# Hybrid decoder block in fp32: the beginning and the end of the FFN's down product in another order, with other raw buffers

## The chip, the cores and the metric

The kernel runs on one core of a Trainium2 chip. The metric is the device time of one execution in microseconds (us). The engines are named as the profile names them: PE (TensorE, matmuls), PEld (its weight loads, which overlap the matmuls), DVE (VectorE), ACT (ScalarE), POOL (GpSimd, here nearly only an issuer of DMAs) and SP (SyncE, which issues DMAs only). [...]

## What is computed

A decoder block for one sequence of 512 tokens with 2048 channels: RMSNorm with a shift and scale from a conditioning vector, two token mixers in parallel (a gMLP gate and a sparse attention), a gated sum, and then a dense SwiGLU FFN. Only the FFN matters here (5632 hidden channels):

```python
h = rms_norm(x1, g_pre_ffn) * (1 + scale) + shift
hid = silu(h @ w_ffn_gate) * (h @ w_ffn_up)          # (512, 5632)
ffn = hid @ w_ffn_down                               # (512, 2048)
out = x1 + gate * rms_norm(ffn, g_post_ffn)
```

## The kernel before

**Arithmetic.** [...] Each operand is divided into a high part `h` (a CAST on ACT) and a low part `l` (a subtraction on DVE), and a product is three matmuls: low by high, high by high, high by low. `split` does that, and the trace shows it as `wh<-...` on ACT (L95) and `wl<-...` on DVE (L79). Both products of the FFN use one level of Strassen's scheme, so that seven quarter products take the place of eight; the sums of quarters that it needs are made on DVE ("fix") and on a few tensors that go through DRAM.

**Steps.** The work of the FFN is a list, `plan`, of `Step`s. A step has a source (`src`, one or two DMA loads of up to 512 KB into a raw buffer, issued on SP), perhaps a `fix` (additions on DVE in the raw buffer), the division into `wh` and `wl`, and the matmuls (`mm`). Hooks place work between steps: `pre` and `post` before and after a step, `late` one step later. `run` walks through the list. Before it emits the matmuls of step i it emits loads and divisions of the steps up to i + `ahead`, and the loads of the steps up to i + `far`; the fix of a step comes two steps before its division. Each engine executes its instructions in the order in which `run` emits them, so `ahead` says what stands in front of what on DVE and ACT:

```python
            for j in range(i, i + st.ahead + 1):
                if st.far:
                    for q in range(i, j + 3):
                        load(q)
                    prefix(j + 2)
                load(j)
                divide(j)
```

**Buffers.** `fetch` gives each step a raw buffer: `wraw`, `xraw` or `draw`, three of each, in a cycle. `divide` does the same for `wh` and `wl`. The `draw` buffers lie in the pool of the down product, which takes the space of operands of the Strassen units before it.

**The FFN's stages.** Unit 0 is computed by `fill`, units 1 to 10 by `strassen(u)`: each makes 512 hidden channels, in four tiles `hn` (tiles 0 and 1, then 2 and 3). Sums of a unit's hidden channels are needed by the down product. `hid_out` transposes the `hn` tiles on PE into a PSUM bank, and `hid_sums` copies from there on ACT (L1523, L1524) and makes four sums on DVE; `sa` and `sb` go to DRAM. For the units 0 to 9 that is done inside the next unit; for the last it is done inside the first steps of the down product, by `mm2` of p = 0 and by the hook `hid_last`.

`down(v)` runs for v = 0 and 1, each a half of the output columns. Its first part has 22 groups p of three steps: `srca` (the hidden sums `sa`), `src1` with `mm1` (weights; fix of two additions with the rows of the third step; result bank A, and B) and `src2` with `mm2` (banks D and C). A group is 24 matmuls of 128 x 512. At the start the order on PE is `mm1` of p = 0 into bank A (6 matmuls), `mm2` of p = 0 into D (6), the 16 transposes of the last unit's `hn` into B and C, `mm1` of p = 1 (6), `mm2` of p = 1 (6), and then the 24 products into B and C of both groups that had been left out. The fix also stores one sum to DRAM (`t2`, by POOL). The second part has 11 groups m of five steps (two loads of `sb`, `mm3` into A, `mm4` into D, `mm5` into C). With the last of them each bank is complete; `late_a`, `late_d` and `post_c` square it on ACT, scale it by `frow` on DVE (`frow` is the FFN's gate row, broadcast to all partitions), and, for v = 1, `d_end` finishes a token tile: the reciprocal root, four multiply-adds of 128 x 512 (`fo<-fo,rd,x`, L86) and the stores of the output. In the last tile the order is A, D, C.

The names of tiles in the trace: `st` is a PSUM bank, `sa_d`, `sb_d`, `t_d`, `t2` are tensors in DRAM, `in_w_dn_dram` the down weights, `in_w_gu_dram` those of gate and up, `gg_d` the gate row.

## Time and profile before

| | before |
|---|---|
| median of three runs | 2617.68 us (2616.56 to 2618.94) |
| profiled execution, own time | 2617.31 us |
| profiled execution, span | 2615.5 us |
| mean granted TensorE clock | 0.992 |
| PE busy | 2546.6 us (97%), 11493 matmuls |
| DVE, ACT busy | 1951.4 us (75%), 1142.7 us (44%) |

The profiled execution's own time is 1.81 us more than its span, which is what lies around the first and last instruction. Starts in the rows below are us from the span's start; the down product begins at about 2158.5 us and ends at 2599.3 us on PE, and the first Strassen unit after `fill` begins at about 1373 us.

### The profile page before, as it was taken

What the parts mean: (1) busy time and instruction counts of PE and PEld (TensorE: products, weight loads), DVE (VectorE), ACT (ScalarE), POOL (GpSimd) and SP (SyncE); (2) the same over time, 40 slices, a digit from 0 to 9 for tenths busy, and PEclk for the clock granted to TensorE, in tenths of its full rate; (3) what the DMA queues carried; (4) which work ended last, traced back from release to release, by engine and by line L of the source; (5) the groups of instructions that cost most, each with busy time, mean ns of one, the idle gap of its engine ahead of it and who ended that gap; (6) DMA issues with size and microseconds to landing.
All of it is one profiled execution on the core that took longest, in us unless ns stands there. A gap on an engine that the chain in (4) does not pass through costs nothing. (4 is left out here: it accounts for less than half of the span.)

```text
span 2615.5 us, 32227 instructions
## 1 busy us (share of the span) xinstructions
PE 2546.6 (97%) x11493; PEld 2103.1 (80%) x11493; DVE 1951.4 (75%) x2678; ACT 1142.7 (44%) x1502; POOL 222.3 (8%) x410
## 2 busy tenths in 40 slices
PE   6999999999999999999998999999999997999997
PEld 4788888888888888888887888888888886888876
DVE  7888654559556777646587788778788777989987
ACT  4432234442343222347564444444444444556554
POOL 0000002110101111000000000000000001000110
PEclk9999999999999999999999999999999998999999
DMA  9886526442426888366746666666666668888996
GB/s 346 312 305 232 177 86 200 143 137 90 136 100 246 300 295 289 127 229 210 259 161 214 213 225 207 209 225 206 197 231 214 205 207 279 299 280 277 297 342 213
DMA packets 194355, 583.30 MB, mean 223 GB/s; under 512 B 21921, under 2 KB 21937, under 8 KB 193297
## 3 DMA queue, kind: packets, MB, share of 16 engines
q1 hardware_dynamic: 152674, 439.65, 50.0%
q0 software_dynamic: 41520, 141.60, 15.3%
q8 instruction: 90, 1.47, 0.2%
q14 instruction: 71, 0.58, 0.1%
HBM read 508.53 MB, written 72.63 MB: 222 GB/s over the span
## 5 line engine op out<-in xcount | busy, mean ns | idle before, releaser
L79 DVE TENSOR_TENSOR wl<-wraw,wh 128x1024 fp32r<-128x1024 f32 (+2 forms) x497 | 596.8, 1212 | 405.4 <-ACT wh L95 392.6
L95 ACT CAST wh<-wraw 128x1024 fp32r<-128x1024 f32 (+2 forms) x497 | 513.5, 1042 | 662.0 <-PE ps L273 202.2
L79 DVE TENSOR_TENSOR wl<-xraw,wh 128x1024 fp32r<-128x1024 f32 (+1 forms) x219 | 258.9, 1204 | 73.6 <-ACT wh L95 72.9
L95 ACT CAST wh<-xraw 128x1024 fp32r<-128x1024 f32 (+1 forms) x219 | 223.4, 1039 | 191.8 <-PE st L1399 102.1
L1399 PE MATMUL st<-wl,Xh 128*128 128x512 f32 x640 | 249.9, 390 | 4.9 <-DVE wl L79 4.9
L1399 PE MATMUL st<-wh,Xl 128*128 128x512 f32 x640 | 251.1, 392 | 3.2 <-ACT wh L95 3.2
L1399 PE MATMUL st<-wh,Xh 128*128 128x512 f32 x640 | 249.3, 390 | 0.0
L1585 PE MATMUL st<-wh,wl 128*128 128x512 f32 x616 | 240.5, 390 | 1.7 <-ACT wh L95 1.7
L1585 PE MATMUL st<-wl,wh 128*128 128x512 f32 x616 | 240.0, 390 | 1.8 <-DVE wl L79 1.8
L1585 PE MATMUL st<-wh 128*128 128x512 f32 x616 | 240.0, 390 | 0.0
L86 DVE SCALAR_TENSOR_TENSOR modw<-modw,cb 128x1024 f32<-128x1024 f32 x192 | 228.2, 1220 | 3.5 <-DMA modw<-in_w_mod_dram 3.1
L271 PE MATMUL ps<-Xh,wl 128*128 128x512 f32 x576 | 229.0, 398 | 0.0
L273 PE MATMUL ps<-Xl,wh 128*128 128x512 f32 x576 | 224.4, 390 | 0.0
L272 PE MATMUL ps<-Xh,wh 128*128 128x512 f32 x576 | 224.2, 389 | 0.0
L1399 PEld LDWEIGHTS st<-wl,Xh 128*128 128x128 f32 x640 | 120.4, 188 | 30.7 <-DVE wl L79 5.7
L1399 PEld LDWEIGHTS st<-wh,Xl 128*128 128x128 f32 x640 | 120.3, 188 | 27.8 <-ACT wh L95 3.6
L1399 PEld LDWEIGHTS st<-wh,Xh 128*128 128x128 f32 x640 | 120.3, 188 | 24.3
L1585 PEld LDWEIGHTS st<-wh,wl 128*128 128x128 f32 x616 | 115.9, 188 | 26.5 <-ACT sa L1524 2.1
L1585 PEld LDWEIGHTS st<-wl,wh 128*128 128x128 f32 x616 | 115.9, 188 | 26.4 <-DVE wl L79 2.2
L1585 PEld LDWEIGHTS st<-wh 128*128 128x128 f32 x616 | 116.0, 188 | 23.8
L272 PEld LDWEIGHTS ps<-Xh,wh 128*128 128x128 f32 x576 | 108.2, 188 | 23.9 <-issue 1.2
L271 PEld LDWEIGHTS ps<-Xh,wl 128*128 128x128 f32 x576 | 108.2, 188 | 23.8 <-issue 1.2
(347 smaller groups left out, 4999.2 us busy)
## 6 DMA issues: line engine op xcount, KB each, us to landing
modw<-in_w_mod_dram SPq DMA_DIRECT2D x100, 512.0 KB, 6.2
modw<-in_w_mod_dram POOLq DMA_DIRECT2D x92, 512.0 KB, 5.7
xraw<-in_w_gu_dram SPq DMA_DIRECT2D x92, 512.0 KB, 4.4
wraw<-in_w_gu_dram SPq DMA_DIRECT2D x68, 512.0 KB, 4.3
wraw<-in_w_out_dram SPq DMA_DIRECT2D x64, 512.0 KB, 3.2
wraw<-in_w_gu_dram SPq DMA_DIRECT2D x118, 256.0 KB, 3.3
t_d<-xraw POOLq DMA_DIRECT2D x67, 256.0 KB, 3.0
wraw<-in_w_ga_dram SPq DMA_DIRECT2D x32, 512.0 KB, 3.4
```

The source lines that it names most:

```text
L79: nc.vector.tensor_tensor(out=o, in0=x, in1=y, op=op)
L86: nc.vector.scalar_tensor_tensor(out=o, in0=x, scalar=s, in1=y, op0=op0, op1=op1, **kw)
L95: nc.scalar.copy(h, src)
L271: nc.tensor.matmul(ps, wl, xh, start=first, stop=False)
L272: nc.tensor.matmul(ps, wh, xh, start=False, stop=False)
L273: nc.tensor.matmul(ps, wh, xl, start=False, stop=last)
L1399: nc.tensor.matmul(bank[t], tok(x, k, t), w[:, ws], start=st, stop=last and w is l, skip_group_check=True)
L1585: nc.tensor.matmul(bank[t], y[:, xs_], w[:, ws], start=first and n == 0, stop=last and n == 2, skip_group_check=True)
```

## The change

The diff does seven things.

1. `fetch`: nine steps of the down product, not six, go into the buffers of the Strassen units before the first `draw` is used. Group p = 2 goes into `xraw`, group p = 3 is the first in `draw`.
2. `sums_end`: the three `xraw` buffers get their place in their pool ahead of the other tiles.
3. In the last unit, `late5` (the product that completes the tiles `hn` 2 and 3) is emitted in `post5`, one step earlier than before.
4. The second `hid_sums` of the last unit writes its `sb` into a part of the tile `x1`, which is empty then, and not into the one `sb` buffer that the first has just used.
5. The load of `frow` (1 MB, issued by POOL) moves from the beginning of the down product to the group p = 6.
6. The look-ahead of the first six steps of the down product is 3, 3, 2, 4, 3, 2, and was 7, 6, 5, 4, 3, 2; loads go ahead by at least six steps.
7. For v = 1 the last two groups change places in part: `mm5` of m = 9 waits until `mm4` of m = 10 is done. Its hidden quarter is loaded again for that (`src22`, two loads of 128 x 256, divided as one of 128 x 512).

```diff
@@ -157,9 +157,9 @@
     more = {"F": 1 << 30, "G": 1 << 30}
 
     def fetch(i):
-        o, g = i - more["F"] - 4, i - more["G"] - 6
+        o, g = i - more["F"] - 4, i - more["G"] - 9
         if g >= 0:
-            o = (more["G"] + 2 - more["F"] + g // 9 * 6 + g % 9 - 3) if g % 9 >= 3 else -1
+            o = (more["G"] + 5 - more["F"] + g // 9 * 6 + g % 9 - 3) if g % 9 >= 3 else -1
         if g >= 0 and g % 9 < 3:
             raw = more["d"].tile([P, 1024], F32, name="draw", tag="draw", bufs=3)
         elif o >= 0 and o % 6 < 3:
@@ -1383,6 +1383,8 @@
         force("sums", lambda: "sums" in B)
         O["hp"].release()
         p = O["xp"] = more["p"] = pool("xp", "right")
+        for _ in range(3):
+            p.tile([P, 1024], F32, name="xraw", tag="xraw", bufs=3)
         O["u2"] = [p.tile([P, 512], F32, name=f"u2{t}") for t in range(2)]
         O["hn1"] = [p.tile([P, 512], F32, name=f"hn1{t}") for t in range(2)]
         b = banks("st")
@@ -1487,6 +1489,8 @@
             def post5():
                 for t in range(2):
                     act(O["u2"][t], B["C"][t], AF.Silu)
+                if u == UNITS - 1:
+                    late5()
 
             def late5():
                 for t in range(2):
@@ -1498,7 +1502,7 @@
                 hid_sums(u - 1, m, B["B"])
 
             plan.append(Step(src5, mm5, fix=fix5, post=post5 if end else None,
-                             late=late5 if end else late6 if m < 2 else None, **kw))
+                             late=late5 if end and u < UNITS - 1 else late6 if m < 2 else None, **kw))
 
     fill(0)
     plan[-1].late = lambda: start("sums", s_chain())
@@ -1519,7 +1523,10 @@
 
         p = O["xp"]
         sa = p.tile([P, 4, HT], F32, name="sa", tag="sa", bufs=2)
-        sb = p.tile([P, 3, HT], F32, name="sb", tag="sb", bufs=1)
+        if (u, i) == (UNITS - 1, 1):
+            sb = E["x1"][:, 0, :3 * HT].rearrange("p (a t) -> p a t", t=HT)
+        else:
+            sb = p.tile([P, 3, HT], F32, name="sb", tag="sb", bufs=1)
         nc.scalar.copy(sb[:, 0:2, :], two(bs[1]))
         nc.scalar.copy(sa[:, 0, :], bs[0][:, :HT])
         tt(sa[:, 2, :], sb[:, 1, :], bs[0][:, HT:], ALU.subtract)
@@ -1537,7 +1544,6 @@
         for n in ("wh", "wl"):
             p.tile([P, 1024], F32R, name=n, tag=n, bufs=3)
         E["row"] = p.tile([P, D], F32, name="frow")
-        gq.dma_start(E["row"], gg_d[16:32].rearrange("a b -> (a b)").partition_broadcast(P))
         E["f"] = p.tile([P, 4, D], F32, name="fo")
         E["x1"] = p.tile([P, 4, D], F32, name="x1")
         E["ssq"] = p.tile([P, 4, 4], F32, name="fssq")
@@ -1589,6 +1595,7 @@
         kw = dict(dur=2.7, ahead=3, far=6)
         w = a["w_dn"][v]
         NP = KF // 2
+        at = {}
         for p in range(NP):
             def keep(h, l, p=p):
                 E["a", p] = h, l
@@ -1639,6 +1646,9 @@
                     return
                 quarter(B["C"], E["a", p], 3, h, l, 1, p == 0, p == NP - 1)
 
+            def row_load():
+                gq.dma_start(E["row"], gg_d[16:32].rearrange("a b -> (a b)").partition_broadcast(P))
+
             def post2():
                 for t in range(2):
                     hn = O["hn1"][t]
@@ -1657,7 +1667,7 @@
             end = p == NP - 1
             plan.append(Step(srca, keep, pre=d_start if v == p == 0 else None, **{**kw, "dur": 0.0}))
             plan.append(Step(src1, mm1, fix=fix1, post=post1 if end else None, late=late1 if end else None, **kw))
-            plan.append(Step(src2, mm2, post=post2 if end else hid_last if v == p == 0 else None, **kw))
+            plan.append(Step(src2, mm2, post=post2 if end else hid_last if v == p == 0 else row_load if v == 0 and p == 6 else None, **kw))
         for m in range(NP // 2):
             end = m == NP // 2 - 1
 
@@ -1676,12 +1686,22 @@
             def src5(raw, m=m):
                 sy.dma_start(raw, t2_d[v % 2][m])
 
-            def fix5(i, raw):
-                tt(raw, raw, loaded[i - 2], ALU.add)
+            def fix5(i, raw, m=m):
+                tt(raw, raw, loaded[at[m]], ALU.add)
 
             def mm5(h, l, m=m, end=end):
                 for j in range(2):
-                    quarter(B["C"], E["a", 2 * m + j], 1, h, l, j, False, end and j == 1)
+                    if v and m == NP // 2 - 2:
+                        quarter(B["C"], E["a22"], j, h, l, j, False, False)
+                    else:
+                        quarter(B["C"], E["a", 2 * m + j], 1, h, l, j, False, end and j == 1)
+
+            def keep22(h, l):
+                E["a22"] = h, l
+
+            def src22(raw, m=m):
+                for j in range(2):
+                    sy.dma_start(raw[:, j * HT:(j + 1) * HT], sb_d[2 * m + j][:, 1, :])
 
             def late_v22():
                 for t in range(2):
@@ -1725,9 +1745,18 @@
                     sy.dma_start(raw[:, :3 * HT], sb_d[p].rearrange("p a t -> p (a t)"))
 
                 plan.append(Step(srcb, keep, n=3 * HT, **{**kw, "dur": 0.0}))
+            at[m] = len(plan)
             plan.append(Step(lambda raw, pair=pair: pair(raw, 1, 0), mm3_, late=late_a if end else None, **kw))
             plan.append(Step(lambda raw, pair=pair: pair(raw, 0, 1), mm4, late=late_d if end else None, **kw))
-            plan.append(Step(src5, mm5, fix=fix5, post=post_c if end else None, late=late_v22 if m == 1 else None, **kw))
+            step = Step(src5, mm5, fix=fix5, post=post_c if end else None, late=late_v22 if m == 1 else None, **kw)
+            if v and m == NP // 2 - 2:
+
+                held = [Step(src22, keep22, n=512, **{**kw, "dur": 0.0}), step]
+            elif v and end:
+                plan.extend(held)
+                plan.append(step)
+            else:
+                plan.append(step)
 
     more["G"] = len(plan)
     for v in range(2):
@@ -1735,8 +1764,8 @@
         down(v)
         for i, st in enumerate(plan[n:]):
 
-            st.ahead = 7 - (i % 3 if i < 66 else (i - 66) % 5) if v or i >= 6 else 7 - i
-            st.far = st.ahead + 2
+            st.ahead = 7 - (i % 3 if i < 66 else (i - 66) % 5) if v or i >= 6 else (3, 3, 2, 4, 3, 2)[i]
+            st.far = max(st.ahead + 2, 6)
 
     begin()
     prep_by(1)
```

On DVE the first place is the beginning of the down product. Before, the rows from the completion of `hn` 0 and 1 (`hn_8621`, `hn_8622`, last unit) to the two `hid_sums` are these (`fssq` is a small tile that is cleared there, `draw<-draw` the fix of p = 2, `sa` and `sb` the tiles of `hid_sums`):

```order
L86 SCALAR_TENSOR_TENSOR hn_8622<-hn_8622,st 128x512
L1545 MEMSET fssq 128x16
L79 TENSOR_TENSOR wl<-wraw,wh 128x1024 x2
L79 TENSOR_TENSOR draw<-draw 128x1024
L79 TENSOR_TENSOR draw<-draw 128x512
L79 TENSOR_TENSOR wl<-wraw,wh 128x1024
L79 TENSOR_TENSOR wl<-draw,wh 128x1024 x2
L86 SCALAR_TENSOR_TENSOR hn_8623<-u_10793,hn_8623 128x512
L86 SCALAR_TENSOR_TENSOR hn_8624<-u_10794,hn_8624 128x512
L79 TENSOR_TENSOR sa<-sb,st 128x256
L79 TENSOR_TENSOR sa<-sa,st 128x256
```

After, the same stretch on DVE reads so (`x_16708` is the tile `x1`, `xraw<-xraw` the fix of p = 2):

```order
L86 SCALAR_TENSOR_TENSOR hn_8623<-u_10796,hn_8623 128x512
L86 SCALAR_TENSOR_TENSOR hn_8624<-u_10797,hn_8624 128x512
L1551 MEMSET fssq 128x16
L79 TENSOR_TENSOR wl<-wraw,wh 128x1024 x2
L79 TENSOR_TENSOR sa<-sb,st 128x256
L79 TENSOR_TENSOR sa<-sa,st 128x256
L86 SCALAR_TENSOR_TENSOR sa<-sa 128x256
L86 SCALAR_TENSOR_TENSOR sb<-sa,sb 128x256
L79 TENSOR_TENSOR sa<-x_16708,st 128x256
```

These follow it directly (the rest of the second `hid_sums`, the fix of p = 2, and the `wl` of `mm2` of p = 1):

```order
L79 TENSOR_TENSOR sa<-sa,st 128x256
L86 SCALAR_TENSOR_TENSOR sa<-sa 128x256
L86 SCALAR_TENSOR_TENSOR x_16708<-sa,x_16708 128x256
L79 TENSOR_TENSOR xraw<-xraw 128x1024
L79 TENSOR_TENSOR xraw<-xraw 128x512
L79 TENSOR_TENSOR wl<-wraw,wh 128x1024
```

The two products that complete `hn` moved from behind the fix and three divisions of later steps to their front, and both `hid_sums` moved ahead of the fix and of the third `wl`.

The second place is the end, again on DVE. Before, the last rows ahead of the first completed bank (`fo<-st,frow`) are these; the last fix is that of `mm5` of m = 10:

```order
L79 TENSOR_TENSOR xraw<-xraw 128x1024
L79 TENSOR_TENSOR wl<-xraw,wh 128x1024 x3
L79 TENSOR_TENSOR wl<-wraw,wh 128x768 x2
L79 TENSOR_TENSOR draw<-draw,wraw 128x1024
L79 TENSOR_TENSOR wl<-wraw,wh 128x1024
L79 TENSOR_TENSOR wl<-draw,wh 128x1024 x2
L86 SCALAR_TENSOR_TENSOR fo<-st,frow 128x512 x2
```

After, the same stretch has the fix and the `wl` of the held `mm5` of m = 9 behind those of `mm3` and `mm4` of m = 10, and the `wl` of the quarter that is loaded again (128 x 512):

```order
L79 TENSOR_TENSOR wl<-draw,wh 128x1024 x2
L79 TENSOR_TENSOR wl<-draw,wh 128x768
L79 TENSOR_TENSOR wl<-wraw,wh 128x768
L79 TENSOR_TENSOR wl<-wraw,wh 128x1024
L79 TENSOR_TENSOR xraw<-xraw,draw 128x1024
L79 TENSOR_TENSOR wl<-wraw,wh 128x1024
L79 TENSOR_TENSOR xraw<-xraw,wraw 128x1024
L79 TENSOR_TENSOR wl<-xraw,wh 128x512
L79 TENSOR_TENSOR wl<-xraw,wh 128x1024 x2
L86 SCALAR_TENSOR_TENSOR fo<-st,frow 128x512 x2
```

What moved there is the work for `mm5` of m = 9, from the front of this stretch to its back. Up to the completion of `hn` 0 and 1 of the last unit the order on every engine is the same as before.

## Rows read from the trace of the kernel before

**Rows 1.** The page, part 1: busy us (share of the span) xinstructions.

```profile
PE 2546.6 (97%) x11493; PEld 2103.1 (80%) x11493; DVE 1951.4 (75%) x2678; ACT 1142.7 (44%) x1502; POOL 222.3 (8%) x410
```

**Rows 2.** Waits of PE, some rows: line, releaser: us in total, times, longest.

```profile
PE st L1516 <- DVE hn L86: 12.9, 1, 12.9
...
PE st L1399 <- DVE wl L79: 4.9, 1, 4.9
...
PE st L1399 <- ACT wh L95: 3.2, 1, 3.2
...
PE st L1585 <- ACT wh L95: 1.7, 1, 1.7
```

**Rows 3.** Timeline of PE, start of the down product: start, length, [idle before <-releaser].

```profile
2161.22 0.38 PE L1516 MATMUL st<-ident,hn 128*128 128x128 f32 x2
2174.54 3.64 PE L1516 MATMUL st<-ident,hn 128*128 128x128 f32 x14 [12.94 <-DVE hn L86]
2177.83 0.78 PE L1585 MATMUL st<-wh,wl 128*128 128x512 f32 x1
...
2184.82 0.47 PE L1585 MATMUL st<-wh,wl 128*128 128x512 f32 x1 [1.68 <-ACT wh L95]
```

**Rows 4.** Timeline of DVE, the same stretch.

```profile
2155.95 1.94 DVE L79 TENSOR_TENSOR wraw<-wraw 128x1024 f32<-128x1024 f32 x2
...
2158.94 1.28 DVE L86 SCALAR_TENSOR_TENSOR hn<-hn,st 128x512 f32<-128x512 f32 x2
...
2160.24 2.36 DVE L79 TENSOR_TENSOR wl<-wraw,wh 128x1024 fp32r<-128x1024 f32 x2
2168.53 1.95 DVE L79 TENSOR_TENSOR draw<-draw 128x1024 f32<-128x1024 f32 x2 [5.92 <-DMA draw<-in_w_dn_dram]
...
2173.80 1.29 DVE L86 SCALAR_TENSOR_TENSOR hn<-u,hn 128x512 f32<-128x512 f32 x2
...
2183.92 0.42 DVE L79 TENSOR_TENSOR sa<-sb,st 128x256 f32<-128x256 f32 x1 [4.97 <-ACT sa L1524]
...
2185.39 1.95 DVE L79 TENSOR_TENSOR xraw<-xraw 128x1024 f32<-128x1024 f32 x2
```

**Rows 5.** Timeline of ACT, the same stretch.

```profile
2159.17 2.93 ACT L95 CAST wh<-wraw 128x1024 fp32r<-128x1024 f32 x3
...
2176.51 0.58 ACT L1523 COPY sb<-st 128x512 f32<-128x512 f32 x1 [4.91 <-PE st L1516]
2176.99 0.38 ACT L1524 COPY sa<-st 128x256 f32<-128x256 f32 x1
```

**Rows 6.** DMA issues, 2156 to 2165 us: tensors, queue, count, KB each, median us to landing.

```profile
frow<-gg_d POOLq DMA_DIRECT2D x1, 1024.0 KB, 9.3
...
draw<-in_w_dn_dram SPq DMA_DIRECT2D x1, 512.0 KB, 5.9
...
xraw<-in_w_dn_dram SPq DMA_DIRECT2D x1, 512.0 KB, 10.1
```

**Rows 7.** Windows: us, busy us of each engine (instructions), PEclk, DMA share, GB/s.

```profile
1372.90:1377.70 4.80, 0.97 (x4) 0.30 (x2) 2.23 (x3) 2.00 (x2) 0.54 (x1) 1.00 0.68 181
1377.70:1387.94 10.24, 5.95 (x14) 4.69 (x15) 9.02 (x9) 4.09 (x4) 1.08 (x2) 0.50 0.69 243
2161.50:2166.18 4.68, 0.10 (x1) 0.00 (x0) 1.10 (x1) 1.64 (x2) 0.00 (x0) 1.00 1.02 353
2166.18:2179.83 13.65, 5.16 (x19) 4.49 (x20) 8.04 (x11) 1.91 (x3) 1.35 (x3) 0.50 0.83 309
2190.00:2240.00 50.00, 50.00 (x222) 41.41 (x221) 49.66 (x49) 27.69 (x28) 4.86 (x9) 1.00 0.88 289
```

**Rows 8.** Timelines of DVE and PE at the end of the program.

```profile
2598.49 0.16 DVE L1210 RECIPROCAL rd<-rd 128x1 f32<-128x1 f32 x1 [0.92 <-ACT rd L89]
...
2609.03 2.74 DVE L86 SCALAR_TENSOR_TENSOR fo<-fo,rd,x 128x512 f32<-128x512 f32 x4
...
2599.09 0.39 PE L1585 MATMUL st<-wl,wh 128*128 128x512 f32 x1
```

## The prediction

> **What bounds the kernel now.** I read the share of busy time first: PE is busy for 2546.6 of 2615.5 us, DVE for 1951.4 [rows 1]. So nothing helps that does not shorten an idle stretch of PE or what lies behind its last matmul. The waits of PE then say where it idles. The longest is one wait of 12.9 us of the transposes at the start of the down product for `hn`, which DVE makes; close behind it come 1.7 us for ACT, and elsewhere there are 4.9 and 3.2 us in one place of the first Strassen unit [rows 2]. Third, the timelines of that stretch. PE does two transposes at 2161.22 and the other fourteen at 2174.54 [rows 3]. DVE shows why: the tiles 2 and 3 of the last unit's `hn` are made at 2173.80, behind a fix that waited 5.92 us for a load and began only at 2168.53 [rows 4]. That fix (p = 2) isn't needed by PE for another three steps. After the transposes `hid_sums` begins on ACT at 2176.51 and ends on DVE at 2185.39, in time for nothing: PE waits once more, for bank C, until 2184.82, with 18 of the 36 matmuls of p = 1 still to come (both starts, 2177.83 and 2184.82, in [rows 3]). At the higher clock level and without waits PE issues 222 matmuls in 50.00 us, 0.225 us each [rows 7]. So p = 1 ends, and `mm1` of p = 2 begins, at 2184.82 + 18 x 0.225 = 2188.9.
>
> The granted clock is the fourth view. PE stopped at about 2161.5; the clock fell to 0.50 at 2166.18 and stayed there until 2179.83, although PE had work again from 2174.54 [rows 3, 7]. Most of the low stretch lies in the wait. Its cost is the work that ran in it: 5.3 us (2174.54 to 2179.83) at half speed, 2.6 us.
>
> Last, the end: the last matmul starts at 2599.09, but DVE has worked without a gap since the reciprocal at 2598.49, which needs bank D, until 2609.03 + 2.74 = 2611.77 [rows 8]. What ends last hangs on when D is ready, not on when C is.
>
> **The change, part by part.** All is worked out on the clock of the profiled execution.
>
> *Start, parts 1, 3, 4 and 6.* `hn` 0 and 1 are done at 2158.94 + 1.28 = 2160.2. The other two now follow at once, 1.29 us [rows 4]: 2161.5. The sixteen transposes need about 0.13 us each (fourteen took 3.64 us at half clock [rows 3], so half of that at full clock): done at 2163.6. On DVE the two `wl` follow (2.36 us [rows 4]): 2163.9. `mm1` of p = 1, six matmuls, goes from 2163.6 to about 2165.0; only its last passes need the second `wl`.
>
> Now `mm2` of p = 1 needs `wh` and `wl` of its weights, and these stand behind `hid_sums`. On ACT: two casts of 0.98 (2.93 for three [rows 5]) end at 2161.1; the copies of the two banks, 0.58 + 0.38 each [rows 5], wait for the transposes and end at about 2164.5; the third cast ends at 2165.5. On DVE: each `hid_sums` takes 2185.39 - 2183.92 = 1.47 us, the fix 1.95, one `wl` about 1.2 [rows 4]: 2163.9 + 2.9 = 2166.8, 2168.7, 2169.9. PE can do two of the six matmuls from 2165.5 (low by high and high by high need only `wh`), and then waits until 2169.9, **about 4.0 us**. From there 28 matmuls are left: 28 x 0.225 = 6.3, so p = 2 begins at 2176.2. Against 2188.9 that is **12.7 us** earlier, at full clock in both places for the part after.
>
> Does the rest of the down product follow? DVE is busy for 49.66 of 50.00 us in its first part [rows 7], so it can't make up for a late start. Its next fix (p = 3) came at 2185.39 [rows 4]; in the new order it follows two `wl` behind 2169.9, at 2172.2, 13.2 us earlier, so it keeps step with PE. Its loads: p = 2 now lies in `xraw`, which group 0 frees when DVE has done its `wl`, from about 2156 to 2159, and not in `draw`, and the 1 MB of `frow` is no longer in that place. With the 5.9 us that a 512 KB load took there [rows 6] the last lands at 2165, before 2166.8. With 10.1 us, the slowest of these rows, it lands at 2169.2, and the fix is 2.4 us late: that is the bound on this side. Group p = 3, now the first in `draw`, can start as p = 2 did before and was there at 2168.53 [rows 4]; it is needed at 2172.2.
>
> *The clock.* PE had a full clock when it stopped, and in both places where it stood still for long the clock fell 4.7 to 4.8 us after the stop: here at 2166.18, and at 1377.70, where there were two stops of 3.2 and 4.9 us with two matmuls between [rows 2, 7]. There fourteen matmuls took 5.95 us instead of 3.15, a loss of 2.8. After the change there is a short stop at 2161.2, two us of light transposes, eight matmuls and the stop of 4.0 us. I think that a fall is likelier than none, and take the loss as between these two: **-2.7 us** against a full clock. In the term of 12.7 the loss of before is included already, so that this one stands against it.
>
> [...]
>
> *Part 2.* The `xraw` buffers lie elsewhere, but their first load waits for the same release as before, that of the whole pool ahead of it, and the order up to the start of the down product is the same. Nothing: the waits of 3.2 and 4.9 us stay [rows 2].
>
> *Part 5.* `frow` goes into the first part of the down product, where the DMA engines have a share of 0.88 at 289 GB/s; in the fullest window they moved 353 GB/s [rows 7]. 1 MB takes 3.0 us at that rate, so no load is more than 3.0 us late, behind a lead of DVE over PE of some 4 us (fix of p = 3 at 2172.2 against `mm1` of p = 2 at 2176.2). Nothing; if the lead were gone, up to 3.0 us.
>
> *Part 7.* `mm5` of m = 9 goes behind `mm4` of m = 10, so D is complete 12 matmuls earlier against the last one: 12 x 0.225 = 2.7 us. The chain of DVE begins that much earlier and C is ready for the third token tile, which DVE reaches 6.9 us after the reciprocal (two tiles of four). The new cast and `wl` of 128 x 512 and the later fixes stand in front of the first `fo`, which costs perhaps 0.3. **2.4 us.** Its bounds are 0 and 2.7: the two loads of 128 KB and a `wl` lie beside PE's work.
>
> **Sum.** 12.7 - 2.7 + 2.4 = 12.4. The profiled execution's own time is 2617.31, which gives 2604.9; the median of the runs is 0.37 above it: **2605.3 us**.
>
> **The rivals.** About 0.2% (5.2 us) is what a measurement of this kernel can tell from no change.
>
> *The clock stays up.* For it: PE stands still for 4.0 us instead of 12.94 and has eight matmuls of work shortly before. Against it: the fall at 1377.70 came after 3.2 us of waiting, two matmuls and a second wait of 1.0 us up to there [rows 7]. 2.7 us less: 2602.6. [...]
>
> *The loads or the end give less.* The fix of p = 2 waits for a load as before (+2.4), or D is not what DVE waits for in the end (+2.4): 2607.7 with one of them, 2610.1 with both. For it speaks that three loads took 5.9 to 10.1 us there [rows 6]; against it that `frow` is gone from the place.
>
> *The change does not do what it says at the start*: another instruction of DVE or a load of p = 3 or 4 holds PE for 8 us or more in the first groups, so that the wait only goes elsewhere: about 2615. DVE's 49.66 of 50.00 us speaks for it, the 13.2 us by which its fix of p = 3 comes earlier against.
>
> *The first Strassen unit is freed too.* If part 2 let its loads start earlier, 3.2 + 4.9 + 2.6 us would go as well: 2594.6. The unchanged order and release speak against it.
>
> *Slower: `frow` in the full stretch.* A weight buffer is loaded again only when the `t2` store out of it has landed, so a late store makes a late load, a late fix and a late store. Were each turn of this loop 3.0 us late and not made up for (DVE has 0.34 us spare in 50), the lead of 4 us would be gone after two groups, and after 6 more groups PE would have lost 18 us, 12.4 + 5.2 and a little: that is the point from which the kernel is slower, at about 2623. Against it: the 64 GB/s that are free in that stretch clear 1 MB in 16 us, three groups. [...]
>
> **How the numbers follow.** My forecast 0.5; the clock stays up 0.2; loads or end give less 0.17; the Strassen unit too 0.03; the wait goes elsewhere 0.06; slower 0.04. Faster by over 0.2%: 0.5 + 0.2 + 0.17 + 0.03 = 0.90; within 0.2%: 0.06; slower: 0.04. The range takes in the first three cases: from 2600.5, the clock up and 2 us of the remaining 4.0 us gone, to 2610.1, both terms lost.
>
> **What would show it.** In the changed kernel's waits of PE the row with 12.9 us is gone and `mm2` of p = 1 waits about 4 us for `wl`. `hn` 2 and 3 end at about 2161.5, the fix of p = 2 starts at about 2166.8 without a wait for a DMA, the clock is low for some us from about 2170, `mm1` of p = 2 starts about 10 us earlier than before, and the first Strassen unit looks the same. At the end the span behind the last matmul is 2.4 us shorter. I'd be wrong if a new wait for a `draw` or `xraw` load appears between 2176 and 2240, or if PE idles around the load of `frow`.

## The result and the profile after

The changed kernel takes 2603.98 us (median of four runs, 2602.49 to 2605.17) against 2618.31 us of the kernel before beside it (four runs, 2616.56 to 2619.55). The ratio is 0.9944, with a 95% interval of 0.9932 to 0.9956: faster by 0.44 to 0.68%. Forecast were 2605.3 us and a gain of 12.4; the gain is 14.3 between the medians and 12.1 between the spans of the two profiled executions (2615.5 and 2603.4).

The waits of PE in the changed kernel. The columns are those of [rows 2]; L1591 and L1401 are the lines L1585 and L1399 of before.

```profile
PE st L1591 <- DVE wl L79: 6.2, 2, 3.9
...
PE st L1401 <- DVE wl L79: 4.7, 1, 4.7
...
PE st L1401 <- ACT wh L95: 3.2, 1, 3.2
```

The wait of 12.9 us and the one of 1.7 us for ACT are gone. In place of them stands one wait of 3.9 us for a `wl`; the second wait of that row, 2.3 us, lies in the second part of v = 1, 11 us after its first matmul, where the kernel before waits 1.8 us. The two waits of the first Strassen unit, 4.7 and 3.2 us, are as before.

The timeline of PE at the start of the down product answers to [rows 3]:

```profile
2159.25 1.91 PE L1520 MATMUL st<-ident,hn 128*128 128x128 f32 x16
2160.92 0.48 PE L1591 MATMUL st<-wh,wl 128*128 128x512 f32 x1
...
2163.40 0.40 PE L1591 MATMUL st<-wh 128*128 128x512 f32 x1
2167.66 0.80 PE L1591 MATMUL st<-wl,wh 128*128 128x512 f32 x1 [3.87 <-DVE wl L79]
...
2172.52 0.62 PE L1591 MATMUL st<-wh 128*128 128x512 f32 x1
2172.95 0.44 PE L1591 MATMUL st<-wl,wh 128*128 128x512 f32 x1
...
2176.66 0.39 PE L1591 MATMUL st<-wh,wl 128*128 128x512 f32 x1
```

All sixteen transposes run at once. Eight matmuls later PE stops, since the third matmul of `mm2` of p = 1 needs the `wl`. From 2167.66 the matmuls stand 0.43 us apart, from 2173.0 again 0.23. `mm1` of p = 2 begins at 2176.66. The timeline of DVE, the answer to [rows 4], shows what stands ahead of that `wl`:

```profile
2158.12 1.28 DVE L86 SCALAR_TENSOR_TENSOR hn<-u,hn 128x512 f32<-128x512 f32 x2
...
2161.61 0.41 DVE L79 TENSOR_TENSOR sa<-sb,st 128x256 f32<-128x256 f32 x1
...
2164.53 1.94 DVE L79 TENSOR_TENSOR xraw<-xraw 128x1024 f32<-128x1024 f32 x2
2166.39 1.22 DVE L79 TENSOR_TENSOR wl<-wraw,wh 128x1024 fp32r<-128x1024 f32 x1
```

`hn` 2 and 3, both `hid_sums` (2161.61 to 2164.53), the fix of p = 2 and the `wl` follow one another without a gap, and the fix does not wait for a load. The windows (columns as in [rows 7], where PEclk is TensorE's granted clock as a share of the full one) give the clock:

```profile
1377.70:1384.53 6.83, 3.33 (x8) 2.66 (x9) 6.41 (x7) 2.31 (x3) 0.64 (x2) 0.50 0.73 264
2163.40:2166.18 2.78, 0.39 (x2) 0.00 (x0) 2.71 (x6) 0.55 (x1) 1.96 (x4) 1.00 1.03 376
2166.18:2173.01 6.83, 5.35 (x13) 4.19 (x14) 5.52 (x6) 2.09 (x2) 1.08 (x2) 0.50 1.00 401
2507.51:2510.93 3.42, 3.42 (x10) 2.65 (x9) 2.71 (x3) 2.04 (x3) 0.00 (x0) 0.50 1.04 416
```

The clock fell while PE stood still and was low for 6.83 us, of which 5.35 us held work. It fell 2.4 us after PE had stopped (2163.80), where [rows 3, 7] have 4.7 to 4.8, so this delay is not the same each time. There is a new low stretch of 3.42 us at 2507.51, behind the wait of 2.3 us. Last, the end of the program, from the timelines of DVE and PE, as in [rows 8]:

```profile
2586.07 0.16 DVE L1210 RECIPROCAL rd<-rd 128x1 f32<-128x1 f32 x1 [0.90 <-ACT rd L89]
...
2596.61 2.74 DVE L86 SCALAR_TENSOR_TENSOR fo<-fo,rd,x 128x512 f32<-128x512 f32 x4
...
2588.93 0.39 PE L1591 MATMUL st<-wl,wh 128*128 128x512 f32 x1
```

DVE's chain begins 2.86 us before the last matmul; before it was 0.60.

Where the 12.1 us between the spans come from, by starts of matmuls in the two timelines of PE (S is the time from the first matmul of p = 0 to the first of p = 2):

| stretch | before | changed | difference |
|---|---|---|---|
| up to the first matmul of the down product | 2158.48 | 2156.46 | -2.0 |
| S | 30.53 | 20.20 | -10.3 |
| p = 2 to the first matmul of v = 1 | 198.63 | 198.64 | 0.0 |
| first part of v = 1 | 119.79 | 119.84 | 0.0 |
| second part of v = 1, first to last matmul | 91.66 | 93.79 | +2.1 |
| start of the last matmul to the end of the span | 16.41 | 14.47 | -1.9 |

### The profile page after: what moved, and what is told of

The parts are those of the page before. It is cut to its first block, busy times and chain, and to the rows that moved or that the text cites. A ratio compares the mean times of both kernels' runs of the same rounds, so it can differ in the third digit from the quotient of the medians.

```text
span 2603.4 us, 32234 instructions
## 1 busy us (share of the span) xinstructions
PE 2547.1 (98%) x11493; PEld 2103.3 (81%) x11493; DVE 1952.3 (75%) x2679; ACT 1143.2 (44%) x1503; POOL 223.1 (9%) x410
## 5 line engine op out<-in xcount | busy, mean ns | idle before, releaser
L1401 PE MATMUL st<-wl,Xh 128*128 128x512 f32 x640 | 249.8, 390 | 4.7 <-DVE wl L79 4.7
L1401 PE MATMUL st<-wh,Xl 128*128 128x512 f32 x640 | 251.1, 392 | 3.2 <-ACT wh L95 3.2
L1401 PE MATMUL st<-wh,Xh 128*128 128x512 f32 x640 | 249.3, 390 | 0.0
L1591 PE MATMUL st<-wl,wh 128*128 128x512 f32 x616 | 241.8, 393 | 6.3 <-DVE wl L79 6.2
L1591 PE MATMUL st<-wh,wl 128*128 128x512 f32 x616 | 241.4, 392 | 0.1
L1591 PE MATMUL st<-wh 128*128 128x512 f32 x616 | 241.4, 392 | 0.0
L1401 PEld LDWEIGHTS st<-wl,Xh 128*128 128x128 f32 x640 | 120.4, 188 | 30.1 <-DVE wl L79 5.2
L1401 PEld LDWEIGHTS st<-wh,Xl 128*128 128x128 f32 x640 | 120.4, 188 | 27.8 <-ACT wh L95 3.6
L1591 PEld LDWEIGHTS st<-wl,wh 128*128 128x128 f32 x616 | 116.7, 190 | 31.6 <-DVE wl L79 7.6
L1401 PEld LDWEIGHTS st<-wh,Xh 128*128 128x128 f32 x640 | 120.4, 188 | 24.2
L1591 PEld LDWEIGHTS st<-wh,wl 128*128 128x128 f32 x616 | 116.7, 189 | 25.4 <-ACT wh L95 0.6
L1591 PEld LDWEIGHTS st<-wh 128*128 128x128 f32 x616 | 116.5, 189 | 24.4
```

The costliest lines, as they stand in the source:

```text
L1401: nc.tensor.matmul(bank[t], tok(x, k, t), w[:, ws], start=st, stop=last and w is l, skip_group_check=True)
L1591: nc.tensor.matmul(bank[t], y[:, xs_], w[:, ws], start=first and n == 0, stop=last and n == 2, skip_group_check=True)
```

## The experiments

The same stretches, from the profile of each kernel, and the time against the kernel before. Each kernel was timed beside its own runs of that one, whose medians were 2617.04 to 2618.31 us; the ratio goes by those:

| kernel | S | p = 2 to v = 1 | second part of v = 1 | end | median us | ratio (95%) |
|---|---|---|---|---|---|---|
| before | 30.53 | 198.63 | 91.66 | 16.41 | 2618.31 | 1 |
| changed | 20.20 | 198.64 | 93.79 | 14.47 | 2603.98 | 0.9944 (0.9932 to 0.9956) |
| u3_late5 | 20.95 | 198.64 | 91.99 | 14.52 | 2605.42 | 0.9953 (0.9938 to 0.9967) |
| u6_ahead | 16.95 | 198.64 | 93.39 | 14.47 | 2602.06 | 0.9938 (0.9923 to 0.9953) |
| u4_sb | 27.36 | 198.64 | 93.63 | 14.58 | 2612.73 | 0.9981 (0.9972 to 0.9991) |
| u1_fetch | 20.31 | 198.62 | 93.74 | 14.51 | 2604.73 | 0.9948 (0.9933 to 0.9963) |
| u257 | 20.17 | 198.63 | 93.81 | 16.49 | 2605.72 | 0.9959 (0.9944 to 0.9974) |
| u36 | 23.08 | 198.63 | 91.95 | 14.50 | 2606.24 | 0.9961 (0.9946 to 0.9976) |
| b3_late5 | 31.97 | 198.63 | 91.39 | 16.38 | 2617.52 | 1.0002 (0.9993 to 1.0012) |
| b34 | 23.90 | 198.62 | 94.38 | 16.42 | 2609.38 | 0.9967 (0.9955 to 0.9980) |
| d4_frow | 20.38 | 200.03 | 93.66 | 14.49 | 2604.57 | 0.9952 (0.9938 to 0.9966) |
| n1_wl | 13.12 | 199.10 | 93.78 | 14.55 | 2598.60 | 0.9931 (0.9916 to 0.9946) |
| n2_x1 | 20.05 | 198.63 | 89.53 | 14.55 | 2599.57 | 0.9936 (0.9922 to 0.9950) |
| n3_both | 13.14 | 199.58 | 89.53 | 14.39 | 2594.07 | 0.9911 (0.9897 to 0.9925) |

Where nothing changes, p = 2 to v = 1 agrees to a few hundredths between profiles, and S to about 0.3 us (20.38 in d4_frow and 20.05 in n2_x1, whose start is that of the changed kernel). So the stretches tell more than the times, whose intervals are 5 to 8 us wide; but each stretch is read from one profile. The theory behind the prediction: DVE executes in order (behind the fix that waited 5.92 us the products for `hn` 2 and 3 began at 2173.80 [rows 4], ahead of it at 2158.12), PE's wait is the sum of what stands ahead of the thing it needs, and a late load counts only for what stands behind it. The rival: one part (the early `hn`, the buffers, the short look-ahead) made the gain alone.

**u3_late5**, the changed kernel with part 3 undone:

```diff
-                if u == UNITS - 1:
-                    late5()
-                             late=late5 if end and u < UNITS - 1 else late6 ...
+                             late=late5 if end else late6 ...
```

> The changed kernel with part 3 undone: the products that complete hn 2 and 3 of the last unit come one step later again. S is the time from the first matmul of mm1 of p = 0 to the first of mm1 of p = 2 on PE: 30.5 us before, 20.2 in the changed kernel. Theory (the wait of 12.9 us came from the fix of p = 2, which stood ahead of hn with a late load): with the short look-ahead only one wl stands ahead of hn 2 and 3, so S grows by 1.0 to 1.5, to 21.2 to 21.7, and the time lies about 1 us above the changed kernel. Rival (this part alone removed the wait): S goes back to 28 or more.

S grew by 0.75, less than the 1.0 to 1.5 expected and far from the rival's 28: with the short look-ahead only one `wl` (1.2 us) stands ahead of `hn` 2 and 3.

**u6_ahead**, the changed kernel with the look-ahead of before:

```diff
-            st.ahead = 7 - (...) if v or i >= 6 else (3, 3, 2, 4, 3, 2)[i]
-            st.far = max(st.ahead + 2, 6)
+            st.ahead = 7 - (...) if v or i >= 6 else 7 - i
+            st.far = st.ahead + 2
```

> The changed kernel with part 6 undone: the look-ahead of the first six steps of the down product is 7, 6, 5, 4, 3, 2 again. DVE then does the fix of p = 2 and three wl ahead of both hid_sums; PE should wait 1.3 us for the wl of mm2 of p = 1 and then for bank B until hid_sums has read it, about 2168.1 on the clock of the changed kernel's profile. Theory (the look-ahead only changes which wait PE has): S is 17.5 to 20.5, so not longer than the 20.2 of the changed kernel. Rival (the short look-ahead is what made the gain): S is 26 or more, the time above 2609.

S is 16.95, 3.25 us shorter than with the short look-ahead: below the expected 17.5. The waits of PE, by its timeline:

```profile
2165.32 0.50 PE L1591 MATMUL st<-wl,wh 128*128 128x512 f32 x1 [1.32 <-DVE wl L79]
...
2168.34 0.47 PE L1591 MATMUL st<-wh,wl 128*128 128x512 f32 x1 [1.83 <-DVE sa L79]
```

They are the two that were expected, 1.3 us for the `wl` and then one for bank B, which DVE's `sa` has to read first. Two stops of 1.3 and 1.8 us with four matmuls between took the place of one of 3.9, and the clock stayed at 1.00 there: behind both the matmuls stand 0.23 to 0.33 us apart, and not 0.43. So part 6, with the other parts in place, is a loss of 3.25 us in S; the medians differ by 1.9 us the same way, which the intervals do not tell from nothing. Part 6 holds two things, the look-ahead of the divisions and that of the loads, and no run takes them apart.

**u4_sb**, the changed kernel with part 4 undone:

```diff
-        if (u, i) == (UNITS - 1, 1):
-            sb = E["x1"][:, 0, :3 * HT].rearrange("p (a t) -> p a t", t=HT)
-        else:
-            sb = p.tile([P, 3, HT], F32, name="sb", tag="sb", bufs=1)
+        sb = p.tile([P, 3, HT], F32, name="sb", tag="sb", bufs=1)
```

> The changed kernel with part 4 undone: the second hid_sums of the last unit writes into the one sb buffer again and has to wait until the first one's store has landed. Theory (in the new order hid_sums stands ahead of the fix of p = 2 and of the wl of mm2 of p = 1, so a wait in it holds everything): the second copy on ACT waits 4 to 6 us, S is 24 to 27, the time 4 to 7 us above the changed kernel. Rival (the store is hidden): S stays at 20.2 within 1.

S grew by 7.2, to 27.36, a little more than expected, and the median by 8.75 us, where 4 to 7 were expected. ACT's timeline shows the wait for the store of the first `sb`, and what stands behind it:

```profile
2168.06 0.59 ACT L1527 COPY sb<-st 128x512 f32<-128x512 f32 x1 [8.64 <-DMA sb_d<-sb]
2168.54 0.38 ACT L1528 COPY sa<-st 128x256 f32<-128x256 f32 x1
2168.80 1.06 ACT L95 CAST wh<-wraw 128x1024 fp32r<-128x1024 f32 x1
```

The copy waits 8.64 us, the `wh` of `mm2` of p = 1 stands behind it, and PE waits for that. Not all of the 8.64 is the store: the wait begins when ACT has made its first copies, and DVE has to make the sums before POOL can issue the store, at 2161.97. The DMA issues say what the store itself took:

```profile
sb_d<-sb POOLq DMA_DIRECT2D x1, 384.0 KB, 6.0
```

**u1_fetch**, the changed kernel with part 1 undone:

```diff
-        o, g = i - more["F"] - 4, i - more["G"] - 9
+        o, g = i - more["F"] - 4, i - more["G"] - 6
-            o = (more["G"] + 5 - more["F"] + g // 9 * 6 + g % 9 - 3) if g % 9 >= 3 else -1
+            o = (more["G"] + 2 - more["F"] + g // 9 * 6 + g % 9 - 3) if g % 9 >= 3 else -1
```

> The changed kernel with part 1 undone: group p = 2 loads into the draw buffers again, which come free with the last Strassen matmul. The fix of p = 2 started at 2164.5 without a wait in the changed kernel. Theory (the late load mattered because hn stood behind it, which it no longer does): the loads land 6 to 9 us after 2156.3, the fix waits 0 to 3 us, S is 20.2 to 23. Rival (the buffers are the main part): the fix waits 5 us or more as before, S is 25 or more.

S is 20.31: the fix of p = 2, now in `draw`, started without a wait, 8.1 us after the first matmul of p = 0. The last of its weights had landed 6.1 us after that matmul. In b34 below, where `frow` is loaded beside it, the same load is issued at the same point, 1.0 us after that matmul, and lands only at 10.1. The DMA issues of u1_fetch and of b34:

```profile
draw<-in_w_dn_dram SPq DMA_DIRECT2D x1, 256.0 KB, 5.0
...
draw<-in_w_dn_dram SPq DMA_DIRECT2D x1, 256.0 KB, 9.0
```

Up to there `frow` is the only DMA that one of them issues and the other does not, so it was `frow` that made the load late.

**u257**, the changed kernel with parts 2, 5 and 7 undone:

```diff
-        for _ in range(3):
-            p.tile([P, 1024], F32, name="xraw", tag="xraw", bufs=3)
...
         E["row"] = p.tile([P, D], F32, name="frow")
+        gq.dma_start(E["row"], gg_d[16:32].rearrange("a b -> (a b)").partition_broadcast(P))
...
-            plan.append(Step(src2, mm2, post=... else row_load if v == 0 and p == 6 else None, **kw))
+            plan.append(Step(src2, mm2, post=... else None, **kw))
...
-                    if v and m == NP // 2 - 2:
+                    if False:
...
-            if v and m == NP // 2 - 2:
+            if False:
...
-            elif v and end:
-                plan.extend(held)
-                plan.append(step)
```

> The changed kernel with parts 2, 5 and 7 undone, which act in three places that the trace keeps apart: the xraw buffers lie where they were, frow is loaded at the beginning of the down product, and mm5 of m = 9 keeps its place. Theory: the two waits of the first Strassen unit stay at 3.2 and 4.7 to 4.9 us (part 2 does nothing); S, the time from the first matmul of p = 0 to that of p = 2, stays at 20.2 within 1 (the 1 MB of frow no longer delays what PE waits for); and the time from the start of the last matmul to the end of the span goes from 14.5 back to 16.4 us (part 7). In all about 2 us above the changed kernel. Rivals: the waits of the Strassen unit differ by over 1 us; or S grows by 3 us or more, since frow delays the loads of p = 2.

All three came as the theory had them, but for a wait of 2.8 us where it had 3.2. The waits of the Strassen unit, by the waits of PE:

```profile
PE st L1399 <- DVE wl L79: 4.7, 1, 4.7
PE st L1399 <- ACT wh L95: 2.8, 1, 2.8
```

4.7 and 2.8 us: the second lies between 2.8 and 3.2 in all fourteen profiles, with part 2 and without, so part 2 does nothing that can be seen. S is 20.17, so `frow` at the beginning costs nothing once p = 2 lies in `xraw`, whose last weights landed here 4.0 us after the first matmul of p = 0. The end is 16.49 us: part 7 is worth 2.0.

**u36**, the changed kernel with parts 3 and 6 undone (both edits above): DVE has the order of before, with the other buffers, `sb` and `frow` of the changed kernel.

> The changed kernel with parts 3 and 6 undone, so that DVE has the order of before, but buffers, sb and frow as in the changed kernel. Theory (half of the wait of 12.9 us came from the late load, half from the work that stood ahead of hn): the fix of p = 2 starts without a wait, hn 2 and 3 are done about 10.6 us after the first matmul of p = 0 (16.6 before), PE waits about 7 us for them, S is 23 to 26. Rival (the order is all): S is 28 to 31. Other rival (the buffers and frow are all): S is 20 to 22.

S is 23.08, as the theory said. PE's wait for `hn` is the one of [rows 2], shorter by 6 us, since the fix ahead of it did not wait:

```profile
PE st L1518 <- DVE hn L86: 6.9, 1, 6.9
```

So of the 10.3 us, 7.5 come without any change of order on DVE, and parts 3 and 6 together give the other 2.9.

**b3_late5**, the kernel before with part 3 alone (the edit of u3_late5 the other way).

> The kernel before with part 3 alone: hn 2 and 3 are completed at once, all else is as before. Theory: the transposes come early, but the fix of p = 2 still waits for its load until 10 us after the first matmul of p = 0, the wl of mm2 of p = 1 is ready 13 us after it, and then both hid_sums follow, the second of which waits for the store of the first sb: PE has the same wait in two other places, S is 25 to 28.5 (30.5 before). Rival (part 3 alone is enough): S is 20 to 22.

S is 31.97, more than the 25 to 28.5 expected and more than before: no gain at all (ratio 1.0002). DVE's timeline shows two waits that took its place:

```profile
2166.09 1.95 DVE L79 TENSOR_TENSOR draw<-draw 128x1024 f32<-128x1024 f32 x2 [4.47 <-DMA draw<-in_w_dn_dram]
...
2180.71 0.42 DVE L79 TENSOR_TENSOR sa<-sb,st 128x256 f32<-128x256 f32 x1 [7.81 <-ACT sa L1526]
```

The second is a wait for ACT, and ACT's timeline says what ACT waited for:

```profile
2179.82 0.58 ACT L1525 COPY sb<-st 128x512 f32<-128x512 f32 x1 [9.90 <-DMA sb_d<-sb]
```

The load holds the fix, and then the second `hid_sums` waits 9.9 us until the store of the first `sb` has landed; the store was issued at 2173.49 and took 6.2 us. In the kernel before it took 3.4 us, and most of that lay beside PE's work. The second copy of ACT came when it had landed, at 2182.93, and the wait of 1.68 us in [rows 3] ends 0.14 us after DVE's last read of that bank (2184.68), which is behind it:

```profile
2183.03 0.58 ACT L1523 COPY sb<-st 128x512 f32<-128x512 f32 x1 [5.66 <-PE st L1585]
```

**b34**, the kernel before with parts 3 and 4.

> The kernel before with parts 3 and 4: hn 2 and 3 are completed at once and the second sb has a place of its own, but p = 2 loads into draw beside frow, and the look-ahead is the long one. The changed kernel without part 6 differs from it in the start of the down product by parts 1 and 5 alone, and had S = 16.95. Theory (together, the buffers and frow decide when the fix of p = 2 can start; either alone was enough to undo without loss only because the short look-ahead asks for the loads later): the fix waits 3 to 5 us for its load, both hid_sums and the wl of mm2 of p = 1 come that much later, S is 20 to 24. Rival (with hn early and sb apart the load no longer matters): S is 17 to 18.

S is 23.90, 8.1 less than with part 3 alone, at the end of the theory's range. The fix still waits for its load:

```profile
2166.09 1.95 DVE L79 TENSOR_TENSOR draw<-draw 128x1024 f32<-128x1024 f32 x2 [4.93 <-DMA draw<-in_w_dn_dram]
```

From here to u6_ahead, whose start differs by parts 1 and 5 alone (and part 2, which does nothing), it is another 6.95 us. PE's two waits there are 6.37 and 0.95 us, against 1.32 and 1.83 in u6_ahead: 4.2 us. The other 2.8 lie in the 28 matmuls from the first of these waits to p = 2, which took 9.65 us without the second wait, against 6.83: the clock fell here, to 0.50 for 10.24 us from 2166.33, and not in u6_ahead.

One reason in the expectation is wrong: the short look-ahead does not ask for the loads later, since those of u1_fetch were issued at the same points. What it puts later is the fix: DVE comes to it 5.2 us after the first matmul of p = 0 here, and at 8.1 in u1_fetch, when the load has landed. That either part 1 or part 5 is enough by itself follows from the landings, at 4.0 (u257) and 6.1 us (u1_fetch), against 10.1 with neither; a run with the long look-ahead and one of the two was not made.

**d4_frow**, the changed kernel with four loads of `frow`:

```diff
-... else row_load if v == 0 and p == 6 else None, **kw))
+... else row_load if v == 0 and 6 <= p < 10 else None, **kw))
```

> The changed kernel with frow loaded four times, after p = 6, 7, 8 and 9, 1 MB each, one per group of 5.4 us. One load in the changed kernel made two loads of weights take 8.0 and 7.9 us instead of about 4.5, and cost DVE 0.6 us. The time from p = 2 to v = 1 on PE was 198.6 us in every kernel so far. Theory (the fear of the prediction's slower rival, with its own bound: a load is late by what lies ahead of it, and PE notices when DVE's lead of some 4 us is gone): DVE loses 0.6 us with the first and about 3 with each further load, PE waits 3 to 8 us in all, 198.6 grows to 202 to 207. Rival (the loads have enough slack): 198.6 within 1. Other rival (the loop of store, load and fix adds up): over 210.

198.6 grew to 200.0, less than the theory's 202 and more than the first rival's 199.6. DVE lost 6.2 us in three waits, by its timeline:

```profile
2210.41 1.95 DVE L79 TENSOR_TENSOR wraw<-wraw 128x1024 f32<-128x1024 f32 x2 [2.00 <-DMA wraw<-in_w_dn_dram]
...
2228.68 1.95 DVE L79 TENSOR_TENSOR wraw<-wraw 128x1024 f32<-128x1024 f32 x2 [2.37 <-DMA wraw<-in_w_dn_dram]
...
2235.89 1.95 DVE L79 TENSOR_TENSOR xraw<-xraw 128x1024 f32<-128x1024 f32 x2 [1.86 <-DMA xraw<-in_w_dn_dram]
```

PE lost 1.4 of them; DVE's lead covered the other 4.8. Each load of `frow` waited until the one before had landed (8.4 us from issue to landing, the median of three), so that the four came over 32 us, which I had not counted.

**n1_wl**, the changed kernel with the `wl` of `mm2` of p = 1 ahead of `hid_sums`, and the fix of p = 2 behind them:

```diff
-                    prefix(j + 2)
+                    if j + 2 != more["G"] + 7 or i > more["G"] + 2:
+                        prefix(j + 2)
...
-            st.ahead = ... else (3, 3, 2, 4, 3, 2)[i]
+            st.ahead = ... else (3, 3, 3, 4, 3, 2)[i]
```

> The changed kernel with one more change: the wl of mm2 of p = 1 is made ahead of both hid_sums, and the fix of p = 2 stays behind them. Theory (the remaining wait of 3.9 us is for work that stands ahead of this wl on DVE, and the low clock comes from that stop): no wait of over 1 us between the transposes and p = 2, the clock stays at its higher level there, S is 12.7 to 14; up to 1.5 us come back in p = 2 and 3, where DVE has no lead. 5.5 to 7.5 us below the changed kernel. Rival (DVE is the bound of this stretch, so that what p = 1 gains is lost behind it): S falls, but the way to v = 1 grows by the same 6 us. Rival on the clock: it falls anyway, S is 16 or more.

S is 13.12 and PE has no stop of over 0.2 us in it, by the window of just that stretch, in which the clock stays at 1.00:

```profile
2154.44:2167.56 13.12, 12.96 (x65) 10.55 (x64) 12.99 (x21) 8.09 (x12) 2.92 (x6) 1.00 0.93 345
```

Behind it 0.5 us come back (199.10): DVE has no lead left, but its group takes less time than PE's, 5.27 us from fix to fix against 5.4. Between the medians the gain is 5.4 us, just under the 5.5 to 7.5 expected.

**n2_x1**, the changed kernel with the loads of `x1` in v = 0:

```diff
-                for t in range(4 if v else 0):
-                    for c in range(4):
-                        gq.dma_start(E["x1"][:, t, c * 512:(c + 1) * 512], x1_d[t][:, c * 512:(c + 1) * 512])
+            def x1_load(m=m):
+                for c in range(2):
+                    t, c = divmod(2 * m - 4 + c, 4)
+                    sy.dma_start(E["x1"][:, t, c * 512:(c + 1) * 512], x1_d[t][:, c * 512:(c + 1) * 512])
...
-            step = Step(..., late=late_v22 if m == 1 else None, **kw)
+            step = Step(..., late=late_v22 if m == 1 else x1_load if v == 0 and m in range(2, 10) else None, **kw)
```

> The changed kernel with the sixteen loads of x1 (4 MB) taken out of the beginning of the second part of v = 1 and spread over the second part of v = 0, two for each group, on SP's queue. Theory (the wait of 2.3 us for a wl at 2504 us and the low clock behind it come from loads that took 12 to 17 us beside x1): no wait there, no low clock, the time from the first matmul of that part to the last is 89.5 to 90.2 us instead of 93.8, and nothing is lost in v = 0 (198.6 from p = 2 to v = 1 stays within 0.5): 3 to 4.5 us below the changed kernel. Rival (v = 0 has no room for 4 MB either): 198.6 grows by 2 us or more.

As the theory said: 89.53 us in the second part of v = 1, and 198.63 in v = 0, 4.4 us between the medians. The edit moves the loads to another queue too, SP's, and this was not taken apart. The wait in the changed kernel begins with a load, on DVE:

```profile
2503.83 1.23 DVE L79 TENSOR_TENSOR xraw<-xraw,wraw 128x1024 f32<-128x1024 f32 x1 [2.64 <-DMA xraw<-t_d]
```

The DMA issues of the changed kernel between 2483 and 2508 us show what had been late:

```profile
x<-x_d POOLq DMA_DIRECT2D x16, 256.0 KB, 9.0
...
xraw<-t_d SPq DMA_DIRECT2D x1, 512.0 KB, 14.1
```

**n3_both**, the edits of n1_wl and n2_x1 together:

> The changed kernel with both: the wl of mm2 of p = 1 ahead of hid_sums, and x1 loaded in v = 0. Theory: the two gains add up, S is 13.1, the second part of v = 1 takes 89.5 to 90.2 us; 9 to 11 us below the changed kernel, ratio to the kernel before about 0.991. Rival: the earlier start moves the transfers of v = 0 into each other, and less than 7 us remain.

The gains add up, but for 0.9 us behind p = 2 (199.58): 2594.07 us, 9.9 below the changed kernel, 0.9911 of the kernel before. No wait of the down product is left over 0.3 us, by the waits of PE:

```profile
PE st L1592 <- DVE fo L86: 0.3, 1, 0.3
...
PE st L1592 <- DVE wl L79: 0.2, 1, 0.2
```

## Why the prediction was right, and where it was not

**The wait at the start (12.7 us, less 2.7 for the clock).** Right in place, cause and size: S fell by 10.3 us where 12.7 - 2.7 = 10.0 was forecast. The remaining wait is 3.87 us (4.0 forecast) for the `wl` behind both `hid_sums` and the fix, and the fix did not wait. u36 and n1_wl show the cause: with DVE's order of before the wait for `hn` is back at 6.9 us, and with the `wl` moved ahead the wait of 3.9 is gone.

**The clock.** It fell, as thought the likelier. The 28 matmuls behind the stop took 9.0 us (2167.66 to 2176.66) against 6.3 at full clock: 2.7 us, the forecast loss, and half of the 5.35 us that held work. Half of the whole low stretch, 6.83 us, would be 3.4: the 1.48 us of it in which PE stood still are not in the loss. n1_wl and u6_ahead show that the loss hangs on the stop: with no stop of over 0.2 us (n1_wl) and with two of 1.32 and 1.83 us (u6_ahead) the clock stayed at 1.00 in this place. The length of a stop alone does not decide it: in u6_ahead a single stop of 1.9 us in the second part of v = 1 was followed by a fall (that part took 93.39 us, and 89.53 without the stop in n2_x1). The prediction's argument against this rival has a slip that changes nothing: at 1377.70 the second wait of the Strassen unit had lasted 0.6 us, counted from the end of the last matmul (1377.07), and not 1.0.

**Parts 1, 3, 4 and 6 as one term.** This was a gap: the prediction summed them, gave no price to any, and did not speak of the store that part 4 gets out of the way. The runs price them by S, each taken out of the changed kernel: part 4 7.2 us, part 3 0.75, part 1 0.1 and part 5 0.0 (nothing, by the scatter of S), and part 6 -3.25. So part 6, which the prediction counts with the gain, takes some of it back. They do not add up to 10.3, since they stand in for one another: part 3 is worth nothing in the kernel before (b3_late5), but 23.08 - 16.95 = 6.1 beside parts 1, 4 and 5 with the long look-ahead; parts 1 and 5 together give 23.90 - 16.95 = 6.95 with the long look-ahead, and singly nothing with the short one, since either gets the load of p = 2 out of the way of `frow`. The sum was right since it followed the whole new order of DVE and ACT row by row.

**The end (2.4 us).** 1.9 in the profile, 2.0 in u257. DVE's last operation ends 10.4 us after the start of the last matmul, and 12.7 before: 2.3, the forecast size. The other 0.3 lie between it and the end of the span (4.1 us, 3.7 before). This last stretch is 4.0 to 4.2 us in all ten profiles with part 7 and 3.7 to 3.8 in the four without. Why it is longer stays open.

**`frow` and the rival that ends slower.** Nothing, as forecast: PE had no wait there, and DVE one of 0.55 us. Two loads of weights beside it took 7.1 and 8.0 us, against 3.7 to 5.5 in the groups around them; `frow` itself took 8.1. The prediction's bound, no load more than 3.0 us late, was a little low: the load of 8.0 us has 256 KB, and the nearest of that size took 3.7 to 4.8. d4_frow shows that four times as much costs PE 1.4 us. The price that the rival gave each turn, 3.0 us, was too high: DVE lost 1.9 to 2.4 in d4_frow, and 0.4 to 1.5 with a single load in the other nine profiles that have it there.

**What the sum did not hold.** Two terms of 2 us with opposite signs. That they cancel in these two profiles, so that 12.1 us come so near to the 12.4 forecast, is luck. The first matmul of the down product lies 2.0 us earlier, but the order ahead of it is the same, and over the fourteen profiles here that start lies anywhere between 2154.4 and 2158.5 us; that of b34, where nothing is changed ahead of it, at 2155.9. It is scatter between executions. A part of it is the low clock in the first Strassen unit, 10.24 us in some profiles, with part 2 (u3_late5, u1_fetch) and without (before, b34), and 6.83 in others. It held 5.95 us of PE's work before and 3.33 after, and half of the difference is 1.3 us. The other term, +2.1 in the second part of v = 1, comes from the wait of 2.3 us (1.8 before) and the low clock behind it. That fall came in eight of the profiles with this wait and was missing in four (before, u3_late5, u36, b3_late5); part 7 isn't its cause, since u257 has it too (93.81), and n2_x1 shows that it goes with the wait. The prediction looked at this place not at all.

## What to carry to other kernels

On an engine that executes in order, as DVE did here (5.92 us of idle time at one fix, with `hn` behind it [rows 4]), write down for each thing that another engine waits for all that stands ahead of it, and ask of each of these whether it has a load or a store to wait for; then move the needed one to the front of the queue, not only the late one away (n1_wl: 7.1 us more from one `wl`). Parts of such a change stand in for one another: taken out one at a time, parts 1, 2 and 5 looked like nothing and part 3 like little, while b3_late5, one of them alone, gained nothing either; only a few combinations showed which wait was behind which. A large transfer that nobody needs yet belongs in a stretch with free bandwidth (281 GB/s in the second part of v = 0, and 348 with 4 MB more) and not at the start of a stage, where the loads that PE needs next are issued beside it (`frow`: a load of 9.0 us instead of 5.0; n2_x1: 4.3 us on PE).

## What the runs showed of the hardware

The store of `sb` (384 KB), right behind that of `sa` (512 KB), took 6.0 and 6.2 us from issue to landing beside loads of weights (u4_sb, b3_late5), and 3.4 in the kernel before. A load of 256 KB took 9.0 us beside the 1 MB of `frow` (b34) and 5.0 without it (u1_fetch), issued at the same point. After a stop of 3.9 us the clock was low each time (the changed kernel, at 0.50 for 6.83 us; u1_fetch, u257, d4_frow, n2_x1: S is 20.05 to 20.38 in all five); after two stops of 1.3 and 1.8 us with four matmuls between it was not (u6_ahead: S is 16.95, the matmuls behind the stops 0.23 to 0.33 us apart). In the second part of v = 1 it fell after single stops of 1.9 us (u6_ahead, 93.39 us for that part) to 2.9 us (b34, 94.38), but not after one of 2.1 us (u36, 91.95). In the second part of v = 0 the DMA engines took 4 MB more, at 348 GB/s instead of 281 in the 70 us from 2290 (windows of n3_both and of the changed kernel), and PE had no wait there.
